# Weight low halves by an accumulating DMA, attention weights in PSUM, denominators on TensorE

## The chip, the cores and the metric

One core of a Trainium2 chip runs the whole program. The metric is device time in microseconds, the median over runs. Engines are named as in the profile: PE (TensorE matmul), PEld (its weight load), DVE (VectorE), ACT (ScalarE), POOL (GpSimd), SP (SyncE). SP, ACT and POOL also issue DMAs from their in-order queues; those of POOL are the "software" queue of the profile.

## The reference

512 tokens and 16 meta tokens (N = 528 rows) of width 1024 pass one block: a token mixer, then a feed-forward layer of 16 experts of which each chooses its 66 rows, each with a residual, then a norm.

```python
u = _rmsnorm(h, norm_g)
proj = u @ w_in        # rq rk rv rg | mq mk mv mo | gates
# four retention heads: q.k scores times a decay in each direction, times v
decay = where(diff >= 0, exp(log_gamma * diff), 0)
ret = forward + backward;   y_ret = head_norm(ret) * silu(rg)
# four mLSTM heads: conv over 5 rows and silu on q, k; then in each direction
s = (q @ k) * exp(log_d - m_row)
num = s @ v;   den = sum(s)
h = num / max(abs(den), exp(-m_row))
y_m = head_norm(sigmoid(mo) * (h_fwd + h_bwd))
y = concat(y_ret, y_m) @ w_out
# experts: router, softmax, top 66 rows of each expert
hid = silu(x_e @ w_gate) * (x_e @ w_up);   out = hid @ w_down * g
```

## The kernel before

Every product is of float32 values split in two: a high half that PE's float32r format holds, and the low rest. Each matmul stands three times, high x high, high x low, low x high, in one PSUM sum.

The mixer works in eight units of one head each, 0 to 3 mLSTM and 4 to 7 retention. A unit has a projection (`prj`), which multiplies four 128-column pieces of `w_in` with the normed input, and an attention (`att`). `weave` takes the generators of a unit's attention and of the next unit's projection in turn, so that PE has projection matmuls to do while an attention step passes through ACT and DVE. Unit 7's attention is woven with the output projection, whose weights are eight further pieces. A scheduler then sets the final order of every engine at build time; each engine and each queue executes its list in order.

A weight piece is 128 x 1024 floats (512 KB). `piece` loads it into a ring of raw buffers (`raws`, left1t in the trace) by a DMA from ACT's queue (line 365), ACT copies the high half to `w_hs` (left2t, line 368), and POOL, for two of the 40 pieces DVE, subtracts it from the raw piece into `w_ls` (left3t, line 369). The two rings of halves hold three pieces, the raw ring two.

An mLSTM attention goes over the two column halves (256 and 272 rows of output) and five row tiles (128, 128, 16, 128, 128). In a tile, `scores` makes a PSUM tile `s` by three matmuls. For each direction ACT makes the exponential (line 520), POOL masks it where the tile meets the diagonal (line 524), DVE multiplies it with `s` (line 526), and `weights_split` makes the high half on ACT (line 478) and the low half on DVE (line 479). `weigh` multiplies both with the values (lines 493 to 495). POOL adds up the weights of each direction (line 509); at the end of a half the two totals are split like weights and summed over the partitions by matmuls with `pick` (line 544), a table that puts each direction's sum in a row of its own. Retention has one direction less: the scores are multiplied with a slice of a table of decays, 128 x 928, that is made for each head (lines 463 to 466).

The high and low halves of the projected features come from `halves`, and the convolution over five rows is five DVE instructions (lines 423 and 426).

PSUM has eight banks: `s` 2, `pj` (projections) 3, `acc` 3.

After the mixer come router and top-k, a chain with little work in each step, and then the experts, whose slabs (704 KB) stream in from SP's queue. They take about 96 to 99 us each.

Of the kernel before, what the change touches and what calls it, by code (L numbers as in the profile page):

```python
# [8 lines left out]
F32 = mybir.dt.float32  # L9
# [109 lines left out]
def token_mixer(tc, a, bcast, left, right, ctx, hold, pp, dr):  # L119
# [4 lines left out]
    def psum(tag):  # L124
        return pp.tile([P, 512], F32, name=tag, bufs=2 if tag == "s" else 3)
# [4 lines left out]
    raws = left.open(lower, 2 * D).ring(2, P, D)  # L130
# [26 lines left out]
    cst_r = left.open(lower, 1472, F32R)  # L157
    pick = cst_r.tile(P, 2 * P - 1)
# [100 lines left out]
    nc.vector.memset(pick[:, P - 1:P].bitcast(F32), 1.0)  # L259
# [67 lines left out]
    sums = left.open(lower, 3 * 272).ring(3, P, 272)  # L327
# [29 lines left out]
    piece_no = itertools.count()  # L357

    def piece(src):
        eng = nc.vector if next(piece_no) in (0, 3) else nc.gpsimd  # L360
# [8 lines left out]
        eng.tensor_sub(l, t, h)  # L369
# [45 lines left out]
    def mlstm_project(p, hd):  # L415
        for s in range(2):
# [6 lines left out]
            nc.vector.tensor_scalar(acc, xq[:, 0:N], conv_w[:, c, 0:1], conv_b[:, c:c + 1],  # L423
                                    op0=ALU.mult, op1=ALU.add)
# [17 lines left out]
    def retention_project(p, hd):  # L442
# [23 lines left out]
        nc.gpsimd.affine_select(dec, dec, pattern=[[1, TW]], base=-OFF, channel_multiplier=-1,  # L466
# [33 lines left out]
    def mlstm_attend(p, hd):  # L500
        num = []
        for l0, ln in HALVES:
# [3 lines left out]
            total, late = [None, None], []  # L506

            def add(d, e, tn):
                nc.gpsimd.tensor_add(total[d][:tn, :ln], total[d][:tn, :ln], e[:tn, :ln])

            for i, (t0, tn) in enumerate(TILES):
                s = scores(p, i, l0, ln)
                for d in range(2):
# [3 lines left out]
                    first = total[d] is None and tn == P  # L517
                    e = next(sums) if first else next(es)
                    ev = e[:tn, :ln]
# [6 lines left out]
                    nc.vector.tensor_mul(ev, s[:tn, :ln], ev)  # L526
                    w = weights_split(e, i, ln)
                    weigh(ps[d], p, i, w, ln, i == use[d][0], i == use[d][-1])
                    if first:
                        total[d] = e  # L530
                        for x in late:
                            add(*x)
                        late = []
                    elif total[d] is None:
                        late.append((d, e, tn))
                    else:
                        add(d, e, tn)
# [609 lines left out]
```

## Time and profile before

| | |
|---|---|
| Median of 3 runs | 2024.74 us (2024.28 to 2026.84) |
| The profiled execution | 2024.38 us; its span 2022.7 us; granted clock 0.981 |
| Start and first projection | 0 to 59 us |
| mLSTM units 0 to 3 | 59 to 242 us, about 46 us each |
| Retention units 4 to 6 | 242 to 335 us, about 31 us each |
| Retention unit 7 and output projection | 335 to 385 us |
| Router, top-k | to about 450 us |
| Experts, final norm | to the end |

The stages of the mixer are cut at the DMAs that carry the denominators (104, 150, 194 and 242 us) and at the first and last pieces of the output weights. The trace gives busy time by engine for any stretch; a row of such a table reads: stretch, its length, then for each engine busy time and number of instructions, the granted clock of PE, the share of the 16 DMA engines and GB/s.

### The profile page before, as it was taken

The page shows a single profiled execution, that of the slowest core. Times are in us where ns is not written, and L with a number is a line of the kernel's source. Part 1 is how long each engine was busy: PE and PEld are TensorE (multiplying, and loading weights), DVE is VectorE, ACT ScalarE, POOL GpSimd, SP SyncE. Part 2 cuts the span into 40 slices and gives each one's busy share as a digit, 9 for nine tenths or more (in the row PEclk, how much of TensorE's full clock was granted, in tenths as well). Part 3 has the DMA queues.
Part 4 walks back from the last instruction along what each step waited for, and adds up shares of the span by engine and source line. Part 5 has one row for each costly group of instructions (what it writes and reads, how often), then busy time and mean ns, then how long its engine had stood idle before and what let it go on. Part 6 is the DMA issues. An engine that isn't in the chain of part 4 may idle for free.

```text
span 2022.7 us, 34626 instructions
## 1 busy us (share of the span) xinstructions
PE 1935.0 (96%) x11841; PEld 1494.8 (74%) x11841; DVE 1793.8 (89%) x2612; ACT 1515.4 (75%) x2398; POOL 335.5 (17%) x301
## 2 busy tenths in 40 slices
PE   7888899959999999999999999999999999999997
PEld 7888899847777777777777767676777776767674
DVE  8999988469999999999999898989898989898988
ACT  4455445358888888888888888888888888888886
POOL 4677764400000000000000000000000000000002
PEclk9999999979999999999999999999999999999998
DMA  4222224698999999999999999999999999999971
GB/s 147 81 64 80 75 75 145 252 345 313 359 365 374 354 381 352 383 351 375 360 366 361 360 358 362 356 364 346 366 343 366 347 365 351 365 352 361 345 254 69
DMA packets 136772, 606.25 MB, mean 300 GB/s; under 512 B 19887, under 2 KB 20527, under 8 KB 136595
## 3 DMA queue, kind: packets, MB, share of 16 engines
q1 hardware_dynamic: 125827, 570.55, 76.1%
q10 hardware_dynamic: 6656, 22.29, 3.2%
q0 software_dynamic: 4112, 11.21, 2.4%
q8 instruction: 92, 1.51, 0.3%
q14 instruction: 85, 0.70, 0.1%
HBM read 593.41 MB, written 10.57 MB: 299 GB/s over the span
## 4 chain that ended last, share of the span: by engine, by line
PE 73%; DVE 2%; ACT 2%; issue 1%; POOL 0%; POOLq 0%; DVEq 0%; ACTq 0%
PE wide L903 16%; PE wide L904 15%; PE wide L905 15%; PE narrow L905 8%; PE narrow L903 8%; PE narrow L904 8%; ACT right5t L888 2%; DVE right5t L889 1%; PE wide L949 1%; PE narrow L949 1%; PE wide L916 1%; DVE left25t L943 0%; DVE left56t L953 0%; ACT wide L1059 0%; POOL right3t L1065 0%
## 5 line engine op out<-in xcount | busy, mean ns | idle before, releaser
L904 PE MATMUL wide<-right5t,left30t 128*66 128x256 f32 (+2 forms) x1984 | 639.2, 327 | 0.0
L903 PE MATMUL wide<-right5t,left30t 128*66 128x256 f32 (+2 forms) x1984 | 624.1, 329 | 5.9 <-ACT right5t L888 1.7
L905 PE MATMUL wide<-right5t,left30t 128*66 128x256 f32 (+2 forms) x1984 | 497.3, 328 | 0.1
L903 PEld LDWEIGHTS wide<-right5t,left30t 128*66 128x66 f32 x1984 | 270.8, 137 | 102.7 <-ACT right5t L888 24.5
L905 PEld LDWEIGHTS wide<-right5t,left30t 128*66 128x66 f32 x1984 | 265.9, 137 | 92.2 <-DVE right5t L889 2.8
L903 PE MATMUL narrow<-right5t,left56t 128*66 128x512 f32 x884 | 307.6, 352 | 2.7 <-ACT right5t L888 2.7
L904 PEld LDWEIGHTS wide<-right5t,left30t 128*66 128x66 f32 x1984 | 270.3, 136 | 52.6 <-issue 0.4
L904 PE MATMUL narrow<-right5t,left56t 128*66 128x512 f32 x884 | 302.4, 352 | 0.0
L905 PE MATMUL narrow<-right5t,left56t 128*66 128x512 f32 x884 | 268.8, 354 | 3.6 <-DVE right5t L889 3.2
L909 POOL DMA_INDIRECT right3t<-u_rows,right3t x16 | 15.7, 981 | 939.0 <-PE narrow L905 457.6
L903 PEld LDWEIGHTS narrow<-right5t,left56t 128*66 128x66 f32 x884 | 122.5, 139 | 58.7 <-ACT right5t L888 3.5
L904 PEld LDWEIGHTS narrow<-right5t,left56t 128*66 128x66 f32 x884 | 122.7, 139 | 55.8 <-issue 3.1
L905 PEld LDWEIGHTS narrow<-right5t,left56t 128*66 128x66 f32 x884 | 114.0, 141 | 57.6 <-DVE right5t L889 12.7
L210 PE MATMUL pj<-right1t,left2t 128*128 128x256 f32 (+1 forms) x512 | 149.3, 292 | 0.6 <-DVE left24t L382 0.6
L212 PE MATMUL pj<-right1t,left3t 128*128 128x272 f32 (+1 forms) x512 | 149.5, 292 | 0.1
L211 PE MATMUL pj<-right2t,left2t 128*128 128x272 f32 (+1 forms) x512 | 148.8, 291 | 0.0
L369 POOL TENSOR_TENSOR left3t<-left1t,left2t 128x1024 fp32r<-128x1024 f32 x38 | 98.4, 2590 | 57.5 <-ACT left2t L368 49.1
L210 PEld LDWEIGHTS pj<-right1t,left2t 128*128 128x128 f32 x512 | 99.5, 195 | 0.8 <-DVE left24t L382 0.7
L212 PEld LDWEIGHTS pj<-right1t,left3t 128*128 128x128 f32 x512 | 99.0, 193 | 0.5 <-DVE left3t L369 0.4
L211 PEld LDWEIGHTS pj<-right2t,left2t 128*128 128x128 f32 x512 | 99.2, 194 | 0.1
L1007 POOL DMA_INDIRECT h_rows<-left31t,right3t x15 | 22.4, 1496 | 415.3 <-ACT left31t L1006 415.3
L943 DVE TENSOR_TENSOR left25t<-wide,left25t 66x512 f32<-66x512 f32 (+1 forms) x96 | 58.5, 637 | 19.2 <-PE wide L905 19.2
(405 smaller groups left out, 4294.9 us busy)
## 6 DMA issues: line engine op xcount, KB each, us to landing
left1t<-in_w_in_f ACTq DMA_DIRECT2D x30, 512.0 KB
left29t<-in_w_gate SPq DMA_DIRECT2D x11, 704.0 KB
left41t<-in_w_gate SPq DMA_DIRECT2D x11, 704.0 KB
left38t<-in_w_gate SPq DMA_DIRECT2D x11, 704.0 KB
left37t<-in_w_gate SPq DMA_DIRECT2D x11, 704.0 KB
left52t<-in_w_up SPq DMA_DIRECT2D x11, 704.0 KB
left51t<-in_w_up SPq DMA_DIRECT2D x11, 704.0 KB
left53t<-in_w_gate SPq DMA_DIRECT2D x10, 704.0 KB
```

The lines of the kernel that those rows point to most:

```text
L210: nc.tensor.matmul(ps[:, :ln], wh, x_h[:, k, l0:l0 + ln], start=(k == 0), stop=False)
L211: nc.tensor.matmul(ps[:, :ln], wh, x_l[:, k, l0:l0 + ln], start=False, stop=False)
L212: nc.tensor.matmul(ps[:, :ln], wl, x_h[:, k, l0:l0 + ln], start=False, stop=(k == KT - 1))
L369: eng.tensor_sub(l, t, h)
L888: nc.scalar.activation(h, src, AF.Copy)
L889: nc.vector.tensor_sub(l, src, h)
L903: nc.tensor.matmul(o, xh, h[:, w], start=start, stop=False)
L904: nc.tensor.matmul(o, xl, h[:, w], start=False, stop=False)
L905: nc.tensor.matmul(o, xh, l[:, w], start=False, stop=last)
L943: nc.vector.tensor_mul(hid[:CAP, s], b[:CAP, :n], hid[:CAP, s])
L949: nc.tensor.transpose(b[:, j * CAP:(j + 1) * CAP], hid[:CAP, f0 + j:SLAB:RH], ident[:CAP, :CAP])
L1007: nc.gpsimd.indirect_dma_start(out=h_rows, out_offset=bass.IndirectOffsetOnAxis(ap=idx_t[:CAP, e:e + 1], axis=0), in_=y, in_offset=None, c ...
```

## The change

Six edits, all in the mixer:

- The low half of a weight piece is made by ACT and a DMA: ACT writes the high half and then a second copy, negated, into the low half's buffer, and an accumulating DMA from POOL's queue adds the raw piece onto it. The raw ring has three buffers.
- The attention weights are not written to SBUF: DVE multiplies into the score tile in PSUM, in place (or into its unused second half; one case stays in SBUF), and both splits read it there.
- The denominators are summed on PE: after each weight tile's values, two matmuls with a two-column slice of `pick` add its column sums to a PSUM tile `den`. POOL's running totals and their splits are gone.
- The decay table of a retention head is made by two exponentials straight from the distances (400 columns each); only the 128 columns in the middle go through POOL, DVE, ACT and POOL.
- High halves of the features, the first convolution tap and the copy of the head's output move from DVE to ACT.
- PSUM: `pj` 2, `den` 1, `s` 2, `acc` 3.

```diff
-        return pp.tile([P, 512], F32, name=tag, bufs=2 if tag == "s" else 3)
+        return pp.tile([P, 512], F32, name=tag, bufs={"s": 2, "pj": 2, "den": 1}.get(tag, 3))
...
-    raws = left.open(lower, 2 * D).ring(2, P, D)
+    raws = left.open(lower, 3 * D).ring(3, P, D)
...
     def piece(src):
-        eng = nc.vector if next(piece_no) in (0, 3) else nc.gpsimd
...
         nc.scalar.activation(h, t, AF.Copy)
-        eng.tensor_sub(l, t, h)
+        nc.scalar.activation(l, t, AF.Copy, scale=-1.0)
+        nc.gpsimd.dma_start(l, t, accum_op=ALU.add)
         return h, l
...
     def halves(fp, scale, p, tag):
-        nc.vector.tensor_scalar(h, fp, scale, None, op0=ALU.mult)
+        nc.scalar.activation(h, fp, AF.Copy, scale=scale)
...
-            nc.vector.tensor_scalar(acc, xq[:, 0:N], conv_w[:, c, 0:1], conv_b[:, c:c + 1],
-                                    op0=ALU.mult, op1=ALU.add)
+            nc.scalar.activation(acc, xq[:, 0:N], AF.Identity, scale=conv_w[:, c, 0:1], bias=conv_b[:, c:c + 1])
...
-        nc.gpsimd.tensor_scalar(dec, dtab, lg[:, H + hd:H + hd + 1], None, op0=ALU.mult)
-        nc.vector.scalar_tensor_tensor(dec, dtab, lg[:, hd:hd + 1], dec, op0=ALU.mult, op1=ALU.min)
-        nc.scalar.activation(dec, dec, AF.Exp)
+        nc.scalar.activation(dec[:, :OFF], dtab[:, :OFF], AF.Exp, scale=back)
+        nc.scalar.activation(dec[:, OFF + P:], dtab[:, OFF + P:], AF.Exp, scale=ahead)
+        mid, dm = dec[:, OFF:OFF + P], dtab[:, OFF:OFF + P]
+        nc.gpsimd.tensor_scalar(mid, dm, back, None, op0=ALU.mult)
+        nc.vector.scalar_tensor_tensor(mid, dm, ahead, mid, op0=ALU.mult, op1=ALU.min)
+        nc.scalar.activation(mid, mid, AF.Exp)
...
-                    nc.vector.tensor_mul(ev, s[:tn, :ln], ev)
-                    w = weights_split(e, i, ln)
+                    if d == 1 or i not in use[1]:
+                        wf = s[:tn, :ln]
+                    else:
+                        wf = s[:tn, ln:2 * ln] if 2 * ln <= 512 else ev
+                    nc.vector.tensor_mul(wf, s[:tn, :ln], ev)
+                    w = weights_split(wf, i, ln)
                     weigh(ps[d], p, i, w, ln, i == use[d][0], i == use[d][-1])
...
+                    for j in range(2):
+                        nc.tensor.matmul(den[:2, :ln], pick[:, 1 - d:3 - d], w[j][:, :ln],
+                                         start=(i, d) == steps[0] and j == 0, stop=(i, d) == steps[-1] and j == 1)
...
-            den = psum("acc")
-            for d in range(2):
-                w = weights_split(total[d], 0, ln)
-                pk = pick[:, P - 1 - d:2 * P - 1 - d]
-                for j in range(2):
-                    nc.tensor.matmul(den[:, :ln], pk, w[j][:, :ln], start=d + j == 0, stop=d + j == 2)
...
-        nc.vector.tensor_copy(nh, n0)
+        nc.scalar.activation(nh, n0, AF.Copy)
...
-                nc.vector.tensor_mul(e[:tn, :ln], s[:tn, :ln], p["dec"][:tn, o:o + ln])
-                w = weights_split(e, i, ln)
+                nc.vector.tensor_mul(s[:tn, :ln], s[:tn, :ln], p["dec"][:tn, o:o + ln])
+                w = weights_split(s, i, ln)
```

The static order of the engines shows where the pieces of the change stand. A row is the line, the operation, what it writes and reads, its shape, and the semaphores that it waits for: an engine's or a queue's, DMAHW for a DMA of a hardware queue, DMASW for one of POOL's. First ACT before, in the first mLSTM unit, from one weight split (line 368) to the next reload of a raw buffer (line 365):

```order
L368 ACTIVATE left2t<-left1t 128x1024 [waits DMAHW0_49,PE_49]
L478 ACTIVATE left18t<-left17t 128x256 [waits DVE_49] x2
L520 ACTIVATE left20t<-left24t,left4t 128x272 [waits DVE_49]
L429 ACTIVATE left24t<-left6t 128x528 [waits DVE_49]
L520 ACTIVATE left17t<-left24t,left4t 16x272 [waits DVE_49,Pool_49]
L365 DMA left1t<-in_w_in_f 128x1024 [waits DMAHW3_49,Pool_49]
L478 ACTIVATE left18t<-left20t 128x256 [waits PE_49,Pool_49]
```

ACT after, at the same kind of place; the split is now lines 364 and 365, the reload 361, silu 425, the weights' high half 478, the exponential 516, the features' high half 384:

```order
L364 ACTIVATE left2t<-left1t 128x1024 [waits DMAHW5_49,PE_49]
L365 ACTIVATE left3t<-left1t 128x1024 [waits PE_49]
L425 ACTIVATE left23t<-left6t 128x528 [waits DVE_49,Activation_49]
L478 ACTIVATE left5t<-s 16x256 [waits DVE_49]
L516 ACTIVATE left17t<-left23t,left4t 128x272 [waits Activation_49]
L478 ACTIVATE left18t<-s 128x256 [waits DVE_49]
L516 ACTIVATE left17t<-left23t,left4t 128x272
L384 ACTIVATE left20t<-left6t 128x528 [waits DVE_49]
L361 DMA left1t<-in_w_in_f 128x1024 [waits DMASW1_49,Activation_49]
L478 ACTIVATE left18t<-s 128x256 [waits DVE_49]
L516 ACTIVATE left17t<-left23t,left4t 16x272
```

The reload waited for POOL and now waits for a DMA of POOL's queue; it stands six activations behind line 365.

POOL before, in the same unit, with the subtraction (369), the running totals (509) and the masks (524):

```order
L509 TENSOR_TENSOR left20t<-left20t,left17t 128x272 [waits DVE_49]
L369 TENSOR_TENSOR left3t<-left1t,left2t 128x1024 [waits DMAHW2_49,PE_49,Activation_49]
L524 AFFINE_SELECT left17t<-left17t 128x272 [waits Activation_49]
L509 TENSOR_TENSOR left20t<-left20t,left17t 16x272 [waits DVE_49]
L524 AFFINE_SELECT left17t<-left17t 128x256 [waits Activation_49]
L509 TENSOR_TENSOR left20t<-left20t,left17t 128x272 [waits DVE_49]
```

POOL after; line 366 is the accumulating DMA, 520 the mask:

```order
L366 DMA left3t<-left1t 128x1024 [waits DMAHW2_49,DMASW2_49,Activation_49]
L520 AFFINE_SELECT left17t<-left17t 128x272 [waits Activation_49]
L520 AFFINE_SELECT left17t<-left17t 128x272 [waits DVE_49,Activation_49]
L520 AFFINE_SELECT left17t<-left17t 128x272 [waits Activation_49]
L366 DMA left3t<-left1t 128x1024 [waits DMAHW3_49,DMASW3_49,Activation_49]
```

Of POOL's list the masks stay; in place of a subtraction stands the issue of a DMA.

PE after, in the first mLSTM unit: the two matmuls for the denominators (530, `den`) follow the weighted sums (493 to 495) of their tile, one behind the high half and one behind the low half:

```order
L493 MATMUL acc<-left18t,left22t 128x256 [waits Activation_49]
L494 MATMUL acc<-left18t,left22t 128x256
L530 MATMUL den<-left18t,left5t 2x256
L486 MATMUL s<-left22t 128x256
L487 MATMUL s<-left22t 128x256
L495 MATMUL acc<-left19t,left22t 128x256 [waits DVE_49]
L530 MATMUL den<-left19t,left5t 2x256
```

They wait for nothing of their own. From the top-k on, the rows of PE, DVE, ACT, SP and POOL are the same in both kernels.

More of the change, by code (lines that the diff above doesn't have):

```diff
@@ L156, in token_mixer @@
     spvs = cst.ring(2, RT, 1, 6)
-    cst_r = left.open(lower, 1472, F32R)
-    pick = cst_r.tile(P, 2 * P - 1)
+    cst_r = left.open(lower, 1220, F32R)
+    pick = cst_r.tile(P, 3)
     center_r = cst_r.tile(P, P)
@@ L258, in token_mixer @@
     nc.vector.memset(pick.bitcast(F32), 0.0)
-    nc.vector.memset(pick[:, P - 1:P].bitcast(F32), 1.0)
+    nc.vector.memset(pick[:, 1:2].bitcast(F32), 1.0)
     for t2h, t2l in w2:
@@ L326, in token_mixer @@
     wtls = left.open(lower, 3 * 272, F32R).ring(3, P, 272)
-    sums = left.open(lower, 3 * 272).ring(3, P, 272)
     set1 = state(lower)
@@ L355, in load_tables @@
         nc.gpsimd.tensor_mul(sinr, sinr, rstd)
-    piece_no = itertools.count()
     def piece(src):
-        eng = nc.vector if next(piece_no) in (0, 3) else nc.gpsimd
         if early:
@@ L462, in retention_project @@
         dec = next(decs)
-        nc.gpsimd.tensor_scalar(dec, dtab, lg[:, H + hd:H + hd + 1], None, op0=ALU.mult)
-        nc.vector.scalar_tensor_tensor(dec, dtab, lg[:, hd:hd + 1], dec, op0=ALU.mult, op1=ALU.min)
-        nc.scalar.activation(dec, dec, AF.Exp)
-        nc.gpsimd.affine_select(dec, dec, pattern=[[1, TW]], base=-OFF, channel_multiplier=-1,
+        ahead, back = lg[:, hd:hd + 1], lg[:, H + hd:H + hd + 1]
+        nc.scalar.activation(dec[:, :OFF], dtab[:, :OFF], AF.Exp, scale=back)
[4 more added lines that the diff above has]
+        nc.scalar.activation(mid, mid, AF.Exp)
+        nc.gpsimd.affine_select(mid, mid, pattern=[[1, P]], base=0, channel_multiplier=-1,
                                 compare_op=ALU.not_equal, fill=2.0)
@@ L505, in mlstm_attend @@
                    for d in range(2)]
-            total, late = [None, None], []
-            def add(d, e, tn):
-                nc.gpsimd.tensor_add(total[d][:tn, :ln], total[d][:tn, :ln], e[:tn, :ln])
+            den = psum("den")
+            steps = [(i, d) for i in range(len(TILES)) for d in range(2) if i in use[d]]
             for i, (t0, tn) in enumerate(TILES):
@@ L516, in mlstm_attend @@
                     full = (t0 + tn - 1 <= l0) if d == 0 else (t0 >= l0 + ln - 1)
-                    first = total[d] is None and tn == P
-                    e = next(sums) if first else next(es)
-                    ev = e[:tn, :ln]
+                    ev = next(es)[:tn, :ln]
                     nc.scalar.activation(ev, p["nmb"][:tn, d, l0:l0 + ln], AF.Exp,
@@ L615, in retention_attend @@
                 s = scores(p, i, l0, ln)
-                e = next(es)
-                nc.vector.tensor_mul(e[:tn, :ln], s[:tn, :ln], p["dec"][:tn, o:o + ln])
-                w = weights_split(e, i, ln)
+                nc.vector.tensor_mul(s[:tn, :ln], s[:tn, :ln], p["dec"][:tn, o:o + ln])
+                w = weights_split(s, i, ln)
                 weigh(ps, p, i, w, ln, i == 0, i == len(TILES) - 1)
```

9 lines of the change are left out of this document (removed).

## The prediction

> **What bounds the kernel now.** I read the page's busy rows, its tenths and its chain first: the change touches only code that runs in the first 400 us, and the question is whether a shift there reaches the end.
>
> ```profile
> PE 1935.0 (96%) x11841; PEld 1494.8 (74%) x11841; DVE 1793.8 (89%) x2612; ACT 1515.4 (75%) x2398; POOL 335.5 (17%) x301
> PE   7888899959999999999999999999999999999997
> DVE  8999988469999999999999898989898989898988
> POOL 4677764400000000000000000000000000000002
> DMA  4222224698999999999999999999999999999971
> PE 73%; DVE 2%; ACT 2%; issue 1%; POOL 0%; POOLq 0%; DVEq 0%; ACTq 0%
> ```
>
> Each digit is a slice of 50.6 us. From slice 10 on PE is full: the experts, a chain on PE. The mixer is slices 0 to 7. There PE stands at 8 and DVE at 8 or 9. The instructions from the top-k on keep their order in the change, so the expert stage has nothing to catch up with or to lose: what the mixer gains or loses appears whole at the end. Hence the sum is made over the mixer, cut where the four mLSTM units, three retention units, and the last unit with the output projection run.
>
> ```profile
> core 0: us, PE busy (x) PEld busy (x) DVE busy (x) ACT busy (x) POOL busy (x), PEclk, DMA share, GB/s
> 0.00:59.00 59.00, 46.12 (x325) 43.11 (x326) 53.02 (x79) 26.05 (x36) 28.56 (x33) 1.00 0.42 140
> 59.00:242.00 183.00, 160.56 (x1178) 152.26 (x1176) 173.33 (x288) 97.03 (x221) 135.63 (x125) 0.96 0.24 71
> 242.00:335.00 93.00, 89.09 (x689) 86.78 (x690) 82.34 (x157) 40.01 (x84) 56.95 (x33) 0.98 0.28 84
> 335.00:385.00 50.00, 49.70 (x399) 48.90 (x398) 29.72 (x61) 20.79 (x37) 18.23 (x14) 1.00 0.75 273
> ```
>
> In the mLSTM row DVE is the fullest (173.3 of 183), ahead of PE. In retention PE leads (89.1 of 93), and in the output stage PE alone is the bound, at 49.70/399 = 0.1246 us a matmul. That is my price of one matmul on a full PE. Sixteen weight pieces pass in the mLSTM row (11.4 us each), twelve in retention (7.75), eight in the output stage (6.25).
>
> Part of DVE's time is not work but interference from POOL:
>
> ```profile
> 126.53 3.29 DVE L479 TENSOR_TENSOR left5t<-left17t,left5t 16x272 fp32r<-16x272 f32 x1
> 127.19 2.33 POOL L369 TENSOR_TENSOR left3t<-left1t,left2t 128x1024 fp32r<-128x1024 f32 x1
> 129.88 0.39 PE L495 MATMUL acc<-left5t,left21t 128*128 128x272 f32 x1 [2.95 <-DVE left5t L479]
> L479 DVE TENSOR_TENSOR left19t<-left17t,left18t x64: 354/428/2662, 73.2 to 366.1; 128x256 fp32r<-128x256 f32 x32, 128x272 fp32r<-128x272 f32 x32
> 59.00:242.00 183.00, 63.44 (x77) 0.96 0.24 71
> L369 POOL TENSOR_TENSOR left3t<-left1t,left2t 128x1024 fp32r<-128x1024 f32 x38 | 98.4, 2590 | 57.5 <-ACT left2t L368 49.1 <-ACT left18t L478 5.4 <-PE pj L212 2.8
> L509 POOL TENSOR_TENSOR left20t<-left20t,left17t 128x256 f32<-128x256 f32 (+3 forms) x44 | 44.3, 1009 | 24.7 <-DVE left19t L479 11.7 <-DVE left17t L526 10.1 <-DVE left4t L405 2.4
> ```
>
> A 16x272 subtraction took 3.29 us while POOL split a weight piece, and PE waited 2.95 us for it. Line 479's median is 0.428, and the fifth row gives its busy time in the mLSTM stage: 63.44 for 77, against 77 x 0.428 = 33.0. So 30 us of DVE there go to overlap with POOL. The change takes away both groups of POOL work shown, 98.4 + 44.3 us.
>
> **The change part by part.**
>
> *DVE, mLSTM.* Gone are the high halves (line 387), conv tap 0 (423), head copies (602) and the splits of the totals (16 of line 479).
>
> ```profile
> 59.00:242.00 183.00, 7.67 (x9) 0.96 0.24 71
> 59.00:242.00 183.00, 5.44 (x6) 0.96 0.24 71
> L602 DVE CAST left15t<-left24t 128x528 fp32r<-128x528 f32 x4 | 2.5, 623 | 0.0
> L479 DVE TENSOR_TENSOR left19t<-left20t,left18t 128x256 fp32r<-128x256 f32 (+1 forms) x32 | 25.7, 809 | 0.5 <-ACT left18t L478 0.5
> ```
>
> The first two rows are lines 387 and 423 in that stage: 7.7 + 5.4, and with three copies (1.9) and 16 x 0.81 = 13.0 the sum is 28. With the 30 us of interference DVE falls from 173 to about 115 of 183: no longer the bound. Reading the weights from PSUM instead of SBUF I price at 0, between the 0.42 us that line 526 needs with a PSUM operand now and the same again.
>
> *PE, mLSTM.* The 32 matmuls of the totals go and 120 two-row ones come: +88. I give each the full 0.1246 (a two-row result streams as many columns), +11 us. The floor is (1178 + 88) x 0.1246 = 157.7, or 9.86 us a piece. No stage with attention ran at its floor: retention was busy 89.09 of 93, so I divide by 0.958: 10.3. PE would then permit 16 x 10.3 = 165 of the 183.
>
> *ACT.* These rows price what comes:
>
> ```profile
> L368 ACT ACTIVATE left2t<-left1t 128x1024 fp32r<-128x1024 f32 x40 | 42.1, 1052 | 11.8 <-PE pj L211 7.8 <-PE pj L662 3.7 <-DMA left1t<-in_w_in_f 0.2
> L429 ACT ACTIVATE left24t<-left6t 128x528 f32<-128x528 f32 x8 | 5.1, 640 | 10.1 <-DVE left6t L426 10.1
> L478 ACT ACTIVATE left18t<-left20t 128x256 fp32r<-128x256 f32 (+1 forms) x32 | 13.3, 417 | 7.9 <-POOL left20t L509 7.5 <-DVE left20t L526 0.2
> 127.55 0.92 ACT L520 ACTIVATE left17t<-left22t,left4t 128x272 f32<-128x272 f32 x2
> ```
>
> In mLSTM: 97.0 + 16 negated copies at 1.05 + 18 passes over 528 columns at 0.64 - 16 total splits at 0.42 = 118.6, or 7.4 us a piece. Two exponentials of 0.51 took 0.92 back to back, 0.1 off for each; with that for all 239 instructions it is 5.9. I take 6.7. In retention: 40.0 + 12.6 + six passes at 0.64 + 0.9 for the decay table in three pieces = 57.3, 4.8 a piece, 3.9 back to back; I take 4.35. The shorter decay table frees DVE and POOL of some 12 us, which here only adds to cover.
>
> *The new wait.* This decides. The reload of a weight buffer is issued from ACT's queue, in order. Today it waits for POOL's subtraction, which is always over:
>
> ```profile
> L365 ACTq EVENT_SEMAPHORE  x25: 17/17/17, 17.2 to 363.6; - x25
> ```
>
> After the change it waits until the accumulating transfer has landed, and it stands behind only six small activations, about 2.7 us, after the copy that starts that transfer. Everything behind it on ACT (exponentials, high halves of the weights) stands still until then, and DVE's subtraction and PE's weighted sums wait for those. The three-deep ring does not help, as it is the order, not the data, that blocks. If the landing takes L after the negated copy, ACT's period for a piece is its work - 2.7 + L. PE's own wait for the low halves is covered: the split runs two pieces ahead, held by PE's use of the ring (the 7.8 us of line 368's row).
>
> No accumulating transfer within SBUF is in the trace. The nearest software-queue rows:
>
> ```profile
> left36t<-in_final_norm_g POOLq DMA_DIRECT2D x1, 512.0 KB, 5.9
> q0 software_dynamic: 144, 0.52, 17.1%
> DMA to landing us min/median/max: 4.3/5.5/9.2
> q0 software_dynamic: 111, 0.27, 16.4%
> DMA to landing us min/median/max: 7.9/8.6/9.8
> q0 software_dynamic: 112, 0.27, 11.7%
> ```
>
> They are a plain 512 KB load (7.5 us window), the 264 KB gather (line 909, 7.5 us window) and the 264 KB accumulating scatter to HBM (line 1007, 12 us window), all beside the full slab stream. Times 16 engines, the load's share is 20.5 engine-us for 128 rows of 4 KB, 0.16 a row; the gather's 0.30, the scatter's 0.34. Accumulating 128 rows at 0.34 is 44 engine-us, 2.7 us on 16. The gather's fixed part is at best 4.3 - 66 x 0.30/16 = 3.1, the load's 5.9 - 1.3 = 4.6. So L lies from 3.1 + 1.3 = 4.4 (no price for accumulating) to 4.6 + 2.7 = 7.3, with the scatter's own 8.6 as the outer end. The mixer's DMA share is 0.24, so I stand near the quiet side: 3.1 + 2.7, and some tenths until POOL reaches it behind a mask, **L = 6.0**; in the output stage (share 0.75) 7.75.
>
> A rule weighed here: the Trainium skill, "DMA: Bandwidth & Descriptors", section "Anatomy of one DMA — SWDGE (gpsimd) path", fits a software DMA by 2.0 us plus bytes over 436 GB/s, 3.2 us for 512 KB. The load row shows 5.9 under contention; by the fit the wait would vanish, and the sum would be the second case below.
>
> *Sum.* mLSTM: ACT 6.7 - 2.7 + 6 = 10.0 a piece beside PE's 10.3; two chains so close and coupled through the weights cost some more, I take 10.7: 171, -12. Retention: 4.35 + 3.3 = 7.65 beside PE's 689 x 0.1246/12 = 7.15 (7.4 with coupling): 7.6, 91.2, -2. Output stage: PE was full and gains nothing; ACT's (20.8 + 8.4)/8 = 3.65 - 2.7 + 7.75 = 8.7 against 6.25 for the five reloads there is +12, of which the two pieces in hand cover about half; the last low half comes 5 us later, mostly covered too: +7. Start: two more activations against a lighter DVE and POOL, 0 (4 either way). Together **-7** on the profiled 2024.38 (its span is 2022.7; the median of the runs is 2024.74): **2017**.
>
> **The rivals.**
>
> *Landing in 5 us or less.* ACT's stall is 2.3 or less, and PE bounds: mLSTM 165 (-18), retention 7.4 x 12 (-4), output +1: 2003. At PE's bare floors (157.7 and 85.8) it is -32: 1992. For it: the quiet queue. Against: the scatter rows.
>
> *ACT's blocked queue decides: slower.* One mechanism, the wait of the reload. At L = 7.5 the periods are 11.5 (184, +1), 9.15 (110, +17), and +12 in the output stage: +30, 2054. At 8.6 it is 12.6, 10.25 and +16: +65, 2089. Retention, which has the least ACT work to lay over the wait, goes first. It decides from L = 6.4, where -12, +2, +8 and the start cancel.
>
> For this rival speaks also a rule of the Trainium skill, "SBUF — State Buffer", section "SBUF: two separate sides": while DVE runs a two-port operation, GpSimd cannot write the descriptors of its own DMAs. No run here shows it.
>
> *The stages do not move.* The score buffers in PSUM (two) are held until both splits are read, and the projection has two instead of three. If PE then waits for buffers as often as it did for DVE, mLSTM stays at 183 and only the output stage's +7 is left: 2024 to 2031. Against: a tile step has 4.6 us (46 us for ten), so two buffers allow 9 us of holding, and multiply, copy and subtraction are 0.42 each.
>
> **How the numbers follow.** A difference under 0.2% (4 us) cannot be told from none. Chances: forecast 0.38 (its own range 2010 to 2023), quick landing 0.22, blocked queue 0.30, unmoved stages 0.10. Faster: 0.27 + 0.22 + 0.01 = 0.50; same: 0.08 + 0.02 + 0.05 = 0.15; slower: 0.03 + 0.28 + 0.04 = 0.35. The range 1994 to 2055 leaves out the very bottom of the quick landing (0.04) and the blocked queue above L = 7.5 (0.14).
>
> **What would show it.** Right: waits of ACT's queue at the reload of about 3 us, thirty times; line 479 near 0.43 throughout; DVE under 130 us of busy time in the mLSTM stage; mLSTM units of 43 us, retention near 31. Reload waits of 17 ns mean the quick landing; waits of 5 us and more, with DVE and PE idle behind ACT, the blocked queue. I am wrong if DVE's subtractions stay at 0.7 us without POOL beside them, if PE waits on the score buffers, or if the experts' order turns out to shift.

## The result and the profile after

The changed kernel takes 2052.6 us (2051.93 to 2053.74, 4 runs) against 2025.79 of the kernel before in the same runs: 1.0129 times, with an interval of 1.0116 to 1.0141. It is 27 us slower. The forecast was 7 us faster. The second rival, the blocked queue, gives 2054 us at a landing of 7.5 us, which is near, but its terms by stage are not the measured ones, as is worked out below. All ratios compare fast runs; three executions far off (4746 and 7908 us of the kernel before, 3137 us of n1_out) are left out.

The page's rows that answer to those of before:

```profile
PE 1948.9 (95%) x11929; PEld 1506.0 (73%) x11929; DVE 1692.5 (82%) x2566; ACT 1557.5 (76%) x2456; POOL 204.6 (10%) x259
PE   7998888859999999999999999999999999999997
DVE  5665556348999999999999898988888989898988
POOL 3223331120000000000000000000000000000002
DMA  7654445878999999999999999999999999999971
PE 78%; DMA 7%; issue 4%; ACT 4%; DVE 4%; POOL 1%; SPq 0%; ACTq 0%; DVEq 0%; POOLq 0%
```

From slice 10 on the rows look as before. In slices 0 to 7 DVE and POOL are relieved, as meant. New is a DMA share of 7% in the chain that ends last. By stages (the row's numbers: stretch, length, busy time and count of PE, PEld, DVE, ACT, POOL, then clock and DMA share):

```profile
59.00:242.00 183.00, 169.49 (x1318) 161.62 (x1318) 112.11 (x259) 116.27 (x243) 54.39 (x82) 0.95 0.52 128
242.00:335.00 93.00, 81.67 (x628) 79.56 (x626) 50.83 (x125) 45.73 (x92) 26.51 (x31) 0.94 0.53 127
335.00:385.00 50.00, 42.74 (x291) 40.02 (x292) 30.19 (x68) 23.51 (x45) 5.20 (x10) 0.90 0.70 203
L479 DVE TENSOR_TENSOR left19t<-s,left18t x72: 357/425/443, 70.2 to 382.7; 128x256 fp32r<-128x256 f32 x40, 128x272 fp32r<-128x272 f32 x32
```

In the mLSTM stretch PE did 1318 matmuls instead of 1178 and DVE fell from 173 to 112 us; the subtraction of line 479, which had run up to 2.7 us in the group of before, now takes 0.443 us at most in the group shown. In retention PE did 628 instead of 689, and in the next 50 us 291 instead of 399, with the granted clock at 0.94 and 0.90 where it had been 0.98 and 1.00. So the work came faster first and slower later.

A second measure is the place of PE in its list of weight pieces: the time of the first matmul of a piece (each input piece has 48, each output piece 42, counted in the trace). All later comparisons use it; the columns are us from the start of the span, in the one profiled execution of each kernel. It shows the projection alone: the attention's matmuls stand between the pieces, in an order that the scheduler sets for each variant. At piece 32 the kernel before has 401 matmuls to do up to the end of the output pieces, the changed kernel and pool_sub 432. At 0.1246 us each these 31 are worth 4 us of any lead.

| kernel | piece 4 | 16 | 24 | 32 | 36 | end of output matmuls | ratio to before, interval |
|---|---|---|---|---|---|---|---|
| before | 49.4 | 180.4 | 262.2 | 336.1 | 365.5 | 387.0 | 1 |
| changed | 53.2 | 163.6 | 264.3 | 337.5 | 382.0 | 414.6 | 1.0129 (1.0116 to 1.0141) |
| plain_copy | 48.7 | 158.7 | 252.8 | 320.6 | 362.5 | 384.8 | 0.9997 (0.9985 to 1.0010) |
| pool_sub | 61.5 | 171.6 | 253.3 | 320.0 | 360.8 | 382.4 | 0.9983 (0.9973 to 0.9993) |
| dve_sub | 54.6 | 164.2 | 242.5 | 320.6 | 365.1 | 387.9 | 1.0001 (0.9991 to 1.0011) |
| out_sub | 54.7 | 165.7 | 264.5 | 334.6 | 379.5 | 401.1 | 1.0088 (1.0068 to 1.0109) |
| reload_sp | 51.7 | 161.3 | 263.2 | 344.8 | 384.6 | 407.8 | 1.0088 (1.0069 to 1.0106) |
| cast_dve | 53.8 | 162.4 | 264.7 | 338.2 | 382.4 | 411.6 | 1.0149 (1.0131 to 1.0167) |
| n1_dve | 52.8 | 165.1 | 253.7 | 332.6 | 377.3 | 400.5 | 1.0074 (1.0058 to 1.0090) |
| n1_out | 53.7 | 165.3 | 253.3 | 331.1 | 376.9 | 398.8 | 1.0077 (1.0059 to 1.0095) |
| pool_bank | 62.2 | 172.3 | 254.5 | 320.2 | 359.5 | 381.0 | 0.9975 (0.9964 to 0.9985) |
| mix_bank | 54.1 | 165.6 | 252.3 | 321.8 | 362.0 | 383.6 | 0.9981 (0.9971 to 0.9991) |
| start_mix | 56.4 | 168.3 | 251.3 | 317.6 | 357.6 | 379.2 | 0.9962 (0.9950 to 0.9973) |
| ratio6 | 58.1 | 168.2 | 250.0 | 318.7 | 366.4 | 387.9 | 1.0007 (0.9998 to 1.0016) |
| no_unit6 | 58.3 | 168.4 | 250.5 | 316.2 | 344.8 | 370.0 | 0.9924 (0.9909 to 0.9940) |
| start_n1 | 58.6 | 166.5 | 243.9 | 309.6 | 349.1 | 370.7 | 0.9925 (0.9911 to 0.9938) |

The changed kernel gains 21 us between pieces 4 and 16, loses 19 between 16 and 24, and loses 26 from piece 32 on: 77 us where 51 were. The attention gains nothing meanwhile: the DMA of unit 3's denominators is issued at 242.2 us before and at 242.6 in the changed kernel, and unit 6's normed output is ready at 347.0 and 356.7.

Where it waits, in the rows of the new instructions (reload, accumulating DMA, and who waited for the landing):

```profile
L361 ACTq EVENT_SEMAPHORE  x34: 17/1012/10872, 16.2 to 373.3; - x34
L366 POOL DMA_DIRECT2D left3t<-left1t x40: 853/882/1219, 9.0 to 396.3; - x40
  POOL left8t L661: 51.8, 8
  ACT left18t L478: 17.7, 5
  ACT left2t L364: 13.8, 3
  PE pj L650: 8.1, 2
DMA to landing us min/median/max: 4.5/5.3/11.4
```

The reload's wait was 17 ns each time; now its median is 1.0 us and its longest 10.9. Of the 37 reloads that follow an accumulate, 33 start within 0.1 us of its landing. The accumulate itself lands 4.5 us after its issue at best (18 of 40 under 5 us), after 5 to 7 in 14 cases, and after 7.1 to 11.4 in eight. Eight are issued more than 1 us after their negated copy is done. Piece 21 shows both at once:

```profile
200.74 1.04 ACT L365 ACTIVATE left3t<-left1t 128x1024 fp32r<-128x1024 f32 x1
203.24 0.19 POOL L577 TENSOR_SCALAR left4t<-left4t 88x6 f32<-88x6 f32 x1 [3.55 <-DMA left4t<-var_d]
204.84 0.92 POOL L366 DMA_DIRECT2D left3t<-left1t  x1
212.06 0.34 ACTq L361 DMA_DIRECT2D left1t<-in_w_in_f  x1
212.44 0.37 ACT L478 ACTIVATE left5t<-s 16x256 fp32r<-16x256 f32 x1 [9.34 <-issue]
212.86 0.58 PE L493 MATMUL acc<-left5t,left20t 128*128 128x256 f32 x1 [5.14 <-ACT left5t L478]
```

The copy ends at 201.8. POOL stands in its queue at the variance's round trip through memory, does one more step of it (1.35 us), and issues the DMA at 204.8, 3.1 us late; the transfer, beside the broadcasts of the denominators and of a variance, takes 7.15 us to land; ACT has nothing to do for 9.3 us, as the reload is next in its queue; and PE stands 5.1 us, since its weights' high half comes from ACT.

### The profile page after: what moved, and what is told of

Same layout as the page of the kernel before. It is cut to its first block, busy times and chain, and to the rows that moved or that the text cites. A ratio compares the mean times of both kernels' runs of the same rounds, so it can differ in the third digit from the quotient of the medians.

```text
span 2052.0 us, 34764 instructions
## 1 busy us (share of the span) xinstructions
PE 1948.9 (95%) x11929; PEld 1506.0 (73%) x11929; DVE 1692.5 (82%) x2566; ACT 1557.5 (76%) x2456; POOL 204.6 (10%) x259
## 4 chain that ended last, share of the span: by engine, by line
PE 78%; DMA 7%; issue 4%; ACT 4%; DVE 4%; POOL 1%; SPq 0%; ACTq 0%; DVEq 0%; POOLq 0%
PE wide L890 16%; PE wide L891 15%; PE wide L892 15%; PE narrow L892 8%; PE narrow L890 8%; PE narrow L891 8%; DMA left3t<-left1t 3%; ACT right5t L875 2%; DVE right5t L876 1%; PE wide L936 1%; PE pj L210 1%; PE pj L211 1%; PE pj L212 1%; PE narrow L936 1%; PE wide L903 1%
## 5 line engine op out<-in xcount | busy, mean ns | idle before, releaser
L891 PE MATMUL wide<-right5t,left29t 128*66 128x256 f32 (+2 forms) x1984 | 639.3, 327 | 0.0
L890 PE MATMUL wide<-right5t,left29t 128*66 128x256 f32 (+2 forms) x1984 | 623.8, 329 | 5.9 <-ACT right5t L875 1.7
L892 PE MATMUL wide<-right5t,left29t 128*66 128x256 f32 (+2 forms) x1984 | 497.1, 328 | 0.1
L890 PEld LDWEIGHTS wide<-right5t,left29t 128*66 128x66 f32 x1984 | 270.7, 137 | 102.6 <-ACT right5t L875 24.8
L892 PEld LDWEIGHTS wide<-right5t,left29t 128*66 128x66 f32 x1984 | 265.9, 137 | 92.1 <-DVE right5t L876 2.8
L890 PE MATMUL narrow<-right5t,left55t 128*66 128x512 f32 x884 | 308.3, 353 | 2.7 <-ACT right5t L875 2.7
L891 PEld LDWEIGHTS wide<-right5t,left29t 128*66 128x66 f32 x1984 | 270.3, 136 | 52.5 <-issue 0.4
L891 PE MATMUL narrow<-right5t,left55t 128*66 128x512 f32 x884 | 302.7, 352 | 0.0
L892 PE MATMUL narrow<-right5t,left55t 128*66 128x512 f32 x884 | 269.5, 355 | 2.8 <-DVE right5t L876 2.4
L890 PEld LDWEIGHTS narrow<-right5t,left55t 128*66 128x66 f32 x884 | 122.9, 139 | 59.2 <-ACT right5t L875 3.5
L891 PEld LDWEIGHTS narrow<-right5t,left55t 128*66 128x66 f32 x884 | 123.0, 139 | 56.4 <-issue 4.3
L892 PEld LDWEIGHTS narrow<-right5t,left55t 128*66 128x66 f32 x884 | 113.7, 140 | 56.5 <-DVE right5t L876 11.5
L210 PE MATMUL pj<-right1t,left2t 128*128 128x272 f32 (+1 forms) x512 | 150.3, 294 | 2.0 <-DVE left23t L379 1.4
L211 PE MATMUL pj<-right2t,left2t 128*128 128x256 f32 (+1 forms) x512 | 149.4, 292 | 0.0
L930 DVE TENSOR_TENSOR left24t<-wide,left24t 66x512 f32<-66x512 f32 (+1 forms) x96 | 58.6, 637 | 19.2 <-PE wide L892 19.2
L364 ACT ACTIVATE left2t<-left1t 128x1024 fp32r<-128x1024 f32 x40 | 42.1, 1054 | 31.5 <-DMA left3t<-left1t 13.8
L994 POOL DMA_INDIRECT h_rows<-left30t,right3t x15 | 22.5, 1502 | 416.0 <-ACT left30t L993 416.0
```

The costliest lines, as they stand in the source:

```text
L210: nc.tensor.matmul(ps[:, :ln], wh, x_h[:, k, l0:l0 + ln], start=(k == 0), stop=False)
L211: nc.tensor.matmul(ps[:, :ln], wh, x_l[:, k, l0:l0 + ln], start=False, stop=False)
L364: nc.scalar.activation(h, t, AF.Copy)
L890: nc.tensor.matmul(o, xh, h[:, w], start=start, stop=False)
L891: nc.tensor.matmul(o, xl, h[:, w], start=False, stop=False)
L892: nc.tensor.matmul(o, xh, l[:, w], start=False, stop=last)
```

## Experiments

**Does the landing cost it?** The same order of instructions on every engine, but without the adding:

```diff
-        nc.scalar.activation(h, t, AF.Copy)
+        nc.scalar.activation(h, t, AF.Copy, scale=0.001)
         nc.scalar.activation(l, t, AF.Copy, scale=-1.0)
-        nc.gpsimd.dma_start(l, t, accum_op=ALU.add)
+        nc.gpsimd.dma_start(l.bitcast(F32), t)
```

> The changed kernel with the same instructions in the same order, but POOL's DMA writes the raw piece over the low half's buffer instead of adding it; to keep the values finite the high half is scaled by 0.001, so the weights are not those of the reference. It measures what the adding itself costs. Theory as in the prediction (an accumulated row costs the DMA engines twice a plain one): landing in 3.2 to 3.6 us against 4.5 where nothing disturbs it, and about a third of the loss back, 2040 us. Rival (the landing is fixed cost): landing within 0.3 us of 4.5 and 2048 to 2053 us.

Landing, minimum, median and maximum, in plain_copy:

```profile
DMA to landing us min/median/max: 2.8/3.2/8.5
```

Against 4.5/5.3/11.4 the adding costs 1.7 us a piece at the minimum and 2.1 at the median. The time falls to that of the kernel before, 0.9997. The expected third was far too little: the adding, with nothing else altered, is worth the whole 27 us. The waits of the reload in ACT's queue add up to 65 us in the changed kernel and to 34 in plain_copy. The adding does not only land later, though. Here are the software queue up to the end of the output pieces and POOL's issue, first in the changed kernel, then in plain_copy:

```profile
q0 software_dynamic: 5824, 21.11, 26.7%
q0 software_dynamic: 5824, 21.11, 13.7%
L366 POOL DMA_DIRECT2D left3t<-left1t x40: 853/882/1219, 9.0 to 396.3; - x40
L366 POOL DMA_DIRECT2D left3t<-left1t x40: 530/576/807, 9.5 to 370.5; - x40
```

The same packets keep the DMA engines busy for 26.7% of 415 us instead of 13.7% of 385, and the issue on POOL takes 0.88 us instead of 0.58. So the adding makes the kernel slow; how much of that is the landing, how much the engines' time that other transfers lack, and how much POOL's, no run separates. And the other parts together with a landing of 3.2 us make nothing faster.

**The parts without the DMA.**

```diff
         nc.scalar.activation(h, t, AF.Copy)
-        nc.scalar.activation(l, t, AF.Copy, scale=-1.0)
-        nc.gpsimd.dma_start(l, t, accum_op=ALU.add)
+        nc.gpsimd.tensor_sub(l, t, h)      # dve_sub: nc.vector
```

> All of the change except the accumulating DMA: the low half of every weight piece is POOL's subtraction again, the negated copy is gone. Theory (the landing of the accumulating DMA, waited for by the in-order queues of ACT and POOL, costs everything): no reload waits left, the mixer's end moves by about -15 to -20 us against before, 2005 to 2012 us. Rival (the other parts lose the time around units 3 to 5, by two projection banks or the longer hold of the score tiles): the loss of 19 us between pieces 16 and 24 stays, and the time is 2025 us or more.

> As the changed kernel, but the low half of every weight piece is a subtraction on DVE (about 1.5 us each, 60 us of the slack that the change made on DVE), no accumulating DMA and no negated copy. Theory: DVE about 140 of 183 us in the mLSTM stage and never beside a long POOL operation, so PE bounds: 1998 to 2006 us, faster than with POOL's subtraction. Rival (PSUM banks or the score tiles' hold): 2025 us or more, as with POOL's subtraction.

0.9983 with POOL, 1.0001 with DVE. The first theory was half right: the loss between pieces 16 and 24 goes (82 and 78 us instead of 101), so two projection banks and the hold of the scores do not make it, and the rival falls for that stretch. But of the 15 to 20 us expected of pool_sub 3.5 are left, and of the 20 or more of dve_sub none. Both lead by 16 us at piece 32 (by 12 and 10 counted in matmuls still to do) and have lost it, all but 5 and none, at piece 36. That is a second question, taken up below.

pool_sub shows one thing more. Its POOL subtracts every weight piece again, 99.0 us in all, and yet DVE's subtraction for the low half of the attention weights (line 478 there) hardly suffers:

```profile
L478 DVE TENSOR_TENSOR left19t<-s,left18t x72: 404/425/443, 70.0 to 361.1; 128x256 fp32r<-128x256 f32 x40, 128x272 fp32r<-128x272 f32 x32
L478 DVE TENSOR_TENSOR left19t<-left17t,left18t x8: 431/442/2426, 96.4 to 225.9; 128x272 fp32r<-128x272 f32 x8
```

Of the 72 that read the PSUM tile `s`, 29 run beside a weight subtraction of POOL and none takes over 0.443 us; of the eight that read an SBUF tile instead, four do, and the longest takes 2.43. So for this line it is the operand in PSUM that ended the interference, not the absence of POOL's work. DVE instructions with both operands in SBUF, such as those of the convolution, still take up to 2.8 us in pool_sub.

**Which queue?** Four edits of the changed kernel, each taking one wait from one queue.

```diff
 reload_sp:  -            nc.scalar.dma_start(t, src)
             +            nc.sync.dma_start(t, src)
 cast_dve:   -                eng = nc.gpsimd if c else nc.vector
             +                eng = nc.vector
 out_sub:    -            wo[dt] = piece(a["w_out"][dt])
             +            wo[dt] = piece(a["w_out"][dt], False)    # POOL subtracts
 n1_dve:     -        nc.gpsimd.tensor_mul(n1, n1, p["rb"][:, 1])
             +        nc.vector.tensor_mul(n1, n1, p["rb"][:, 1])
```

> The changed kernel with the reload of the raw weight buffers issued from SP's queue instead of ACT's; nothing else is altered. Theory (ACT's in-order queue, blocked at each reload until the accumulate has landed, is a main part of the loss): ACT has no reload waits left, pieces 16 to 24 take 85 us or less instead of 101, and the time falls by 8 to 15 us, to 2038 to 2045. Rival (POOL's queue and the landing itself cost it, or the wait only moves to SP, in front of the small DMAs that carry denominators and variances): within 4 us of 2052, or slower.

> The changed kernel with the copy of the low halves of the eight output pieces (128x128) on DVE instead of POOL, so that POOL's queue no longer waits for a landing before it issues the next accumulate; the wait for the landing goes to DVE's queue. Theory (POOL's cast holds the accumulates of pieces 36, 38 and 39 back by 2.9, 1.0 and 6.7 us): no accumulate of the output stage is issued more than 1 us after its negated copy, and 5 to 10 us come back: 2042 to 2047. Rival (the landings of 10 us beside the slab stream decide, whoever waits): 2049 to 2055.

> The changed kernel with POOL's subtraction for the eight output pieces only; the 32 input pieces keep the accumulating DMA. Theory (in the output stage POOL's cast of the low half waits for each landing and holds back the next accumulate, and landings beside the slab stream take 10 us): the output stage goes back from 77 us (pieces 32 to the end) to 51 to 55, the time to 2027 to 2032 us. Rival (the stage is long because unit 7's attention or the slab stream makes it so): it stays above 65 us, 2045 us or more.

> The changed kernel with the second multiplication by the reciprocal denominators (line 586) on DVE instead of POOL, so that POOL does not stand waiting for the round trip of the denominators in front of an accumulate. Theory (POOL's in-order queue issued the accumulates of pieces 21 and 26 late by 3.1 and 4.3 us): those two are issued within 1 us of their negated copy, pieces 16 to 28 take 10 us less than 137, and the time falls to 2042 to 2047. Rival (the landing itself, 7 us beside the 528 KB broadcasts of the denominators, or DVE's own wait for that round trip, sets it): 2049 to 2055.

reload_sp came 8 us down, to 1.0088, but not where it was expected: pieces 16 to 24 still take 102 us, and the gain is in the output stage. In SP's queue the reload stands ahead of the small DMAs of the denominators (its longest wait there was 18 us), so the wait moved, as the rival had it, though not without gain. cast_dve gained nothing (1.0149): no accumulate of that stage is issued late any more, yet three of the last five still land after 9.9 to 10.9 us. So POOL's cast is where the wait shows, not what makes it. out_sub also came to 1.0088, 11 us above the expected range: the last four pieces take 21.6 us instead of 32.7, but pieces 32 to 36 remain at 45. n1_dve gains 11 us (1.0074; its interval overlaps those of the two runs at 1.0088): pieces 21 and 26 are issued 0.3 us after their copies, and pieces 16 to 28 take 129 us instead of 137. The instruction that stood in POOL's queue in front of piece 26, in the changed kernel:

```profile
259.09 1.81 POOL L586 TENSOR_TENSOR left21t<-left21t 128x528 f32<-128x528 f32 x1 [9.66 <-DMA left21t<-rden_d]
262.00 0.91 POOL L366 DMA_DIRECT2D left3t<-left1t  x1
```

By piece 32 n1_dve is 5 us ahead of the changed kernel, and it gains 9.5 more in the last four pieces (23.2 us instead of 32.7). Line 586 does not run there. No accumulate of that stage is late any more in n1_dve, and only two land after more than 9 us; why moving an earlier instruction did this, no run shows.

**Do the two repairs add?**

> The changed kernel with both repairs together: line 586 on DVE, and POOL's subtraction for the eight output pieces; the 32 input pieces keep the accumulating DMA. Theory (the two losses, POOL's queue behind the round trips with 11 us and the output stage's landings with 9 to 12, are separate and add): 2028 to 2033 us, within 10 us of the variant without any accumulating DMA (2023). Rival (they overlap, or a third wait takes their place): 2036 us or more.

They do not: 1.0077, no better than n1_dve alone, as the rival had it. With line 586 moved, the last four pieces already take 23.2 us, and what is left lies at pieces 16 to 36, where reloads still wait 3 to 7 us. That the output stage's late landings were in part a consequence of the earlier delay fits this, but is not shown.

**Where does the lead of 16 us go?** pool_bank gives every third output tile the free bank of the denominators, mix_bank and start_mix move some subtractions to DVE, and ratio6 changes the weave.

```diff
-        ps = psum("pj")
+        ps = psum("den" if (2 * dt + i) % 3 == 2 else "pj")     # pool_bank and all below
...
+        eng = nc.vector if next(piece_no) in (0, 3) else nc.gpsimd     # start_mix; mix_bank: 0, 3 to 19
...
-            weave(tc, att(u), prj(u + 1), 3.8 if units[u][0] == "m" else 5, hooks)
+            weave(tc, att(u), prj(u + 1), 3.8 if units[u][0] == "m" else 6, hooks)     # ratio6
```

> The change without the accumulating DMA (POOL subtracts) and with a third PSUM bank for the output projection: every third tile of it takes the bank of the denominators, which is free by then. Theory (the lead of 16 us that the other parts have at piece 32 is given back between pieces 32 and 36, as two banks let PE prepare only two output tiles before it waits for the last retention norm): pieces 32 to 36 take 33 to 36 us instead of 41, and 5 to 8 us come off: 2015 to 2018. Rival (the chain of unit 6's norm and unit 7's scores sets that stage whatever PE could do meanwhile): within 2 us of 2023.

> As the one with the third bank, but DVE subtracts pieces 0, 3 and 4 to 19 (the mLSTM units, where it was 10 us quicker than POOL by piece 20) and POOL the others (in retention POOL was quicker). Theory: 8 to 10 us ahead of POOL alone at piece 20, kept until piece 32, and with the bank part of it kept to the end: 2008 to 2014. Rival (the lead runs into the same chain before piece 36): 2018 to 2024.

> The variant with POOL's subtraction and the third bank, with the subtractions of pieces 0 and 3 on DVE as in the kernel before. Theory (POOL alone starts 12 us late at piece 4, and from there to piece 32 PE is full, so what the start gains stays): piece 4 at 50 to 54 us instead of 62, and 2013 to 2018 us. Rival (a lead is given back to the chain of the last two retention units whatever its source, as with the mixed variant): 2019 to 2024 us.

> As start_mix, with six instead of five projection steps woven with each step of a retention attention, which moves the second output piece in PE's order some 20 matmuls later. Theory: the time goes with where the output pieces stand in the order, within 4 us of start_mix either way. Rival (the weave sets the retention stage): more than 6 us apart.

The bank is worth little: 0.9975 against 0.9983, the intervals overlap; pieces 32 to 36 take 39 us, not 33 to 36. mix_bank, 7 us ahead of pool_bank at piece 16, is level with it by piece 32 (0.9981). start_mix, at piece 4 after 56.4 us and not the 50 to 54 expected, keeps 2 of its 6 us: 0.9962, an interval that overlaps that of pool_bank. ratio6 is 9 us slower than start_mix, against the expected 4 at most, nearly all of it between pieces 32 and 36 (48 us instead of 40), so the order of attention and projection counts. The decisive one leaves out the wait for unit 6:

```diff
-        order = (4, 5, 6, 7, 0, 1, 2)
+        order = (4, 5, 6, 7, 0, 1, 1)
```

> As start_mix, but the output projection takes head 1 twice and leaves out head 2, so that its first tiles do not wait for the last norm of retention unit 6; the output is not the reference's. Theory (that wait, beside unit 7's attention, is where a lead of 18 us at piece 32 falls to 8 by piece 36): PE has work from 317 us on, pieces 32 to 36 take 32 to 35 us instead of 40, and 5 to 8 us come off: 2011 to 2014. Rival (unit 7's attention chain alone sets the end of that stage): within 3 us of 2019.

Busy times in the same 15 us (PE is the first, with its number of matmuls), start_mix first, then no_unit6:

```profile
328.00:343.00 15.00, 11.49 (x69) 10.24 (x68) 11.15 (x26) 6.78 (x16) 2.73 (x2) 0.77 0.70 253
328.00:343.00 15.00, 15.00 (x123) 14.92 (x123) 13.22 (x28) 6.80 (x15) 5.92 (x4) 1.00 0.65 212
```

With the wait PE does 69 matmuls at a granted clock of 0.77, without it 123 at 1.00. Pieces 32 to 36 take 28.6 us, less than the 32 to 35 expected, and the time is 2011.9, in the expected range. Some 3.5 of the 11 us less in that stretch are order: the new schedule puts 28 of its 259 matmuls behind piece 36. So the lead is given back there: projection and output pieces run ahead, but the seventh factor of every output tile is unit 6's normed output, and that comes at the end of a chain of attention, variance, square root and reciprocal.

The places in the trace agree. Unit 6's normed output is ready at 347.0 us before, 337.2 in pool_sub and 335.7 in start_mix: 10 and 11 us earlier, where the first output matmul is 16 and 18 earlier. Until it is ready PE can do six factors of as many tiles as there are banks, 54 matmuls before and in start_mix, 36 in pool_sub. In the kernel before it has 11 us to fill with them and with attention, in pool_sub 17 and in start_mix 18. In ratio6, slower by 9 us, the normed output is ready at 349.1.

**One more edit, on both sides.**

> As start_mix with line 586 on DVE. Without an accumulating DMA nothing waits behind POOL's multiplication but masks and subtractions, so the theory expects little: 2014 to 2020 us. Rival (POOL's wait for the denominators costs as much as with the accumulating DMA): 2008 to 2012 us.

> The kernel before with its multiplication of line 598 moved from POOL to DVE, and nothing of the change. It tells whether the 7 us that this move gained in start_n1 belong to the changed parts. Theory (in the kernel before DVE is the fullest engine, so one more DVE instruction in each mLSTM unit costs what POOL's wait gave): 2022 to 2030 us. Rival (POOL's wait for the denominators was as dear before): 2016 to 2020 us.

Line 586 on DVE in start_mix gives 2012.06 us, 0.9925: 15 us faster than before, against the theory and at the edge of the rival's range, and 7 more than start_mix. In start_mix POOL stood at that instruction (there line 588) for 13.5 us, with its masks and subtractions behind it:

```profile
POOL left23t L588 <- DMA left23t<-rden_d: 7.9, 2, 5.9
POOL left21t L588 <- DMA left21t<-rden_d: 5.6, 2, 3.9
```

Without it pieces 16 to 24 take 77 us instead of 83, and unit 6's normed output is ready at 327.5 us instead of 335.7. So the wait was dear even without an accumulating DMA. The same edit in the kernel before gives nothing, 1.0002 (0.9993 to 1.0011). So the gain needs the changed parts. That it needs them because DVE has room there is the theory of that run; nothing isolates it.

## Why the prediction was wrong

The prediction's sum has four terms. By the pieces that begin in each of its stages before (the first six, sixteen, ten, and the last eight with the end of the output matmuls) they came out so:

| stage | forecast | changed | pool_sub | plain_copy |
|---|---|---|---|---|
| start | 0 | +2 | +12 | -2 |
| mLSTM | -12 | -11 | -22 | -15 |
| retention | -2 | +10 | -6 | +2 |
| output | +7 | +26 | +11 | +13 |

- **The output stage, +7: the step that failed most.** "PE was full and gains nothing", and two pieces in hand would cover half of the reloads' +12. It was +26. Some 11 of it come without any accumulating DMA (pool_sub): unit 6's norm sets the pace, as no_unit6 shows, and a lead of the projection is lost within four pieces. I had read the output stage of before (PE 49.70 of 50) as bound by PE. It was, because there the norm is ready 11 us after the first output matmul and PE has work until then; in pool_sub it is 17. The other 15 come with the accumulating DMA, whose landings there take up to 11.4 us.
- **Retention, -2: the second step that failed.** It was +10, where plain_copy has +2, so the adding costs 8 us there. Which wait makes them stays open: neither n1_dve nor reload_sp shortens that stretch (102 and 108 us against 101). The row that the prediction divides by twelve holds ten; six pieces, not four, begin before 59 us. PE's floor there is 689 x 0.1246/10 = 8.6 us a piece and not 7.15. ACT's work is shared by ten as well, so the term would have stayed near nothing.
- **mLSTM, -12: the number came, in the projection alone.** By the denominators' DMAs the four units end at 242.6 us instead of 242.2, 45 us each and not the 43 named as a sign of being right. Entering it as a gain to the end was the error that the first bullet tells.
- **DVE, mLSTM: the number was right, the reason not.** DVE was forecast at 115 and came to 112 us. The 30 us of interference were put down to POOL's work and expected to go with it. In pool_sub that work is back, and the subtractions that read PSUM stay at 0.425 us. The prediction priced the operand in PSUM at nothing, and for line 479 it is what took the interference away.
- **PE, mLSTM: right.** PE ran pieces 8 to 16 in 79 us, 9.9 a piece against the 10.3 allowed, but with 76.5 matmuls a piece and not 79. Per matmul that is 0.129 us, and 0.1246/0.958 = 0.130 was allowed.
- **L, the landing: right on average, wrong in kind.** I took one number, 6.0 (7.75 in the output stage). From the end of the negated copy to the landing it was 5.8 us on average in pieces 4 to 19, 6.3 in 20 to 31, 8.8 in 32 to 39; but single ones went from 4.8 to 18. The reload did not wait "about 3 us, thirty times": half of its 34 waits are about 1.0 us or less, and the longest 10.9. A mean hid the cases that decide.
- **"Some tenths until POOL reaches it behind a mask": too little.** POOL's queue also holds the multiplication with the denominators, the variance steps and, in the output stage, the cast of the low half, and each of them waits for a DMA. I had counted what stands behind the reload on ACT, but not what stands ahead of the accumulate on POOL. Eight accumulates are issued 1.0 to 6.7 us after their copies. n1_dve measures one of these instructions at 5 us by piece 32 and 11 in the end.
- **The third rival, unmoved stages:** its cause, the PSUM banks, is refuted by pool_sub up to piece 32, but its outcome, that the gain does not reach the end, is what the other parts alone show.
- **The break-even at L = 6.4:** plain_copy stands at break-even, and there the landing comes 3.8 us after the negated copy in the median and 4.6 on average. The place of 6.4 followed from a sum in which the gain was kept.
- **The rule of the Trainium skill,** "DMA: Bandwidth & Descriptors", section "Anatomy of one DMA — SWDGE (gpsimd) path": its 3.2 us for a plain transfer of 512 KB is the median that plain_copy shows. I set it aside for a contended row of 5.9. It holds for a plain transfer; the adding costs 1.7 to 2.1 us on top, where I had worked out 1.4 from the scatter's rows. So this rival, the quick landing, failed on the adding and on what lay beside it.
- The other rule of the Trainium skill, "SBUF — State Buffer", section "SBUF: two separate sides", of DVE's two-port operations that keep GpSimd from writing descriptors, is not decided: issues took 0.85 to 1.22 us, and no run separates this from other causes.

Beside the landings of 7 us and more stand 528 KB broadcasts (of the denominators once, of another row table, `nmb_d`, twice), the loads at the start, and the slabs. That these cause them is read from the times in the trace; no run took them away.

## What to carry to other kernels

A DMA that produces an operand is an instruction with a latency of 3 to 11 us; before it is put in, list for each in-order queue what stands ahead of its issue and what stands behind the wait for its landing, and look there for instructions that wait for other DMAs. A gain in one stage counts only up to the next chain of dependences: ask what the engine that is freed will run into, and try that by taking the dependence away. Where two streams of work are woven, follow both: in the changed kernel the projection was 17 us ahead at piece 16 and the attention not at all. And test a replacement operation apart from the edits that come with it: here the rest of the change with POOL's subtraction is 0.2% faster than the kernel before, and 0.75% with a third bank for the output tiles, two subtractions on DVE and one multiplication moved.

## What the runs showed of the hardware

- Adding into SBUF by a DMA of 512 KB lands in 4.5 us at best, the plain copy in 2.8. Beside other transfers the adding takes up to 11.4 us (DMA share 0.94 meanwhile), the plain copy up to 8.5 (share 0.90).
- An added row of 4 KB keeps a DMA engine busy for 0.34 us in the median, a copied one for 0.16. These are the two prices that the prediction took from the scatter's and the load's rows.
- A PE that has waited runs slower for a while. In start_mix it does 30 matmuls in 4 us, then all but stands for 3 us, and then needs 5.53 us for 23; the granted clock falls from 1.00 to 0.53:

```profile
325.00:329.00 4.00, 3.68 (x30) 3.30 (x28) 2.59 (x8) 1.79 (x6) 0.00 (x0) 1.00 0.12 46
329.00:332.00 3.00, 0.29 (x2) 0.00 (x0) 2.61 (x6) 1.52 (x5) 0.00 (x0) 0.80 0.97 315
332.00:338.00 6.00, 5.53 (x23) 4.94 (x24) 4.83 (x12) 1.82 (x5) 0.00 (x0) 0.53 0.40 122
```

- So a wait costs more than its gap: in the changed kernel pieces 32 to 36 have 6.2 us of gaps, but take 15 us more than before for 31 more matmuls (3.9 us at 0.1246).
- A 16x272 subtraction of two SBUF tiles on DVE beside a long POOL operation took 3.29 us, and in the changed kernel none takes over 0.43. With one operand in PSUM a subtraction takes at most 0.443 us beside POOL's subtractions too (pool_sub). In the kernel before, the interference cost line 479 some 30 of DVE's 173 us in the mLSTM stage.
